# A sixth tile for the running block sums, earlier requests for block loads, four small buffers, and the fourth block's additions taken out of program order

## The chip, the cores and the metric

The kernel runs on one core of one Trainium2 chip. The metric is the time of one execution in microseconds (us), the median of several runs. Five engines of the core matter here: PE (TensorE, matrix products), ACT (ScalarE), DVE (VectorE), POOL (GpSimd, here mostly a queue that issues transfers, among them the ones that add to what lies in SBUF) and SP (SyncE, a second queue that issues transfers).

## The reference

One decoder layer on 256 tokens of width 2048, all in float32. The part that matters is the combined input projection:

```python
h = rmsnorm(x, pre_norm_g[l])
proj = h @ w_in[l]
(a_q, a_k, a_v, a_g, a_lr, b_q, b_k, b_v, b_g, m_a, m_b) = jnp.split(proj, offsets, axis=-1)
...
merged = jax.nn.sigmoid(m_a) * y_a + jax.nn.sigmoid(m_b) * y_b
out = merged @ w_out[l]
x = x + rmsnorm(out, post_norm_g[l])
```

The columns of `proj` feed a gated linear attention (`a_*`), a differential attention (`b_*`) and two merge gates (`m_*`). The two attentions give `y_a` and `y_b` by two further products with 2048 x 2048 weights.

## The kernel before

**Float32 as two halves.** Every weight tile is used as a rounded part `hi` and a remainder `lo`. In `emit_half` ACT writes `hi` (line 354, a copy that rounds, 128 x 1024) and DVE writes `lo` (line 355, the tile minus `hi`). PE multiplies `hi` with both parts of the activations and `lo` with the rounded part alone. One such pair of 128 x 1024 is called a half below. `hi`, `lo` and the raw tile each rotate through three buffers, and halves are prepared three ahead of PE (`AHEAD`, in `take`).

**The joined phase.** Nine stretches of 1024 columns (`SETS`, the sets 0 to 8) are not multiplied directly. Each is cut into four blocks of 1024 x 512 and computed with seven block products in place of eight. `PRODUCTS` gives their order: 1, 3, 5, 6, 2, 7, 4. Each block product has two parts `t` of two halves `h`, and a half takes six matmuls of 128 x 512. A block is held as two tiles of 128 x 2048 (1 MB), one for each `t`.

Some products need sums of blocks, and these are formed in place in running tiles (the tag `chain`, five buffers of 1 MB):

- the two tiles `a` are loaded with block 0 and used by product 1. Block 1 is then added by a transfer (`accumulate`, line 249, on POOL's queue) for product 5. Block 3 is then added by DVE out of the tiles `b` for product 6. Block 2 is added by DVE after that, for product 4.
- the two tiles `b` are loaded with block 3 and used by product 3. After DVE has added them to `a`, block 1 is added to them by a transfer, for product 7.
- block 2 alone is held in tiles `c`, which product 2 uses.

`follow_set` issues what follows a half. After the halves of product 5, part 1, it adds block 3 to the tile `a` of part 0; after those of product 6, part 0, to the tile `a` of part 1 (line 257; each addition is 128 x 1024). After the halves of product 7 the same line adds block 2. `emit_set` asks for the tiles of the next set through `link` (lines 222 to 228): `a` part 0 ahead of product 2, `a` part 1 ahead of product 7 part 1, `b` part 0 and `b` part 1 ahead of the two parts of product 4. A request takes a buffer of the tag; with five buffers and four in use by the set, the first request finds one free and each later one needs a buffer that the running set gives back.

**What runs beside the sets.** Between the halves of the sets come 64 halves of ordinary products (`others`): the last value columns, the keys and queries of the linear attention, and a part of those of the differential attention. `phase_steps` lists the order; a set takes 28 halves of its own and, from set 1 to set 7, seven of these. Small results wait in tiles `t2` (line 172, six buffers of 256 KB in this phase): sums of products (`p1`, `p5`, `p35`), and the queries and keys of the differential attention with their rounded parts (`dq`, `dk`, `dh`) until POOL has stored them.

**What sets the order of work.** Each engine runs its instructions in the order of its queue. That order is made ahead of time by a planner, which walks through the program with its own estimate of times. When an engine is free in that plan, it takes the instruction that comes first in the program among those whose inputs are ready. `keep_in_program_order` pins an instruction behind the one written just before it for the same engine. An instruction that isn't pinned may be taken ahead of others that are not ready yet. In `follow_set` all additions are pinned, and so are the transfers on POOL's queue. In the phase the matmuls are pinned too.

When the phase ends, the buffers of `blocks` and `first` (with `chain` and `t2`) are given up, and other pools take their space.

Of the kernel before, what the change touches and what calls it, by code (L numbers as in the profile page):

```python
# [6 lines left out]
F32 = mybir.dt.float32  # L7
# [4 lines left out]
ALU = mybir.AluOpType  # L12
AX = mybir.AxisListType

P = 128
# [127 lines left out]
def hybrid_kernel(ctx: ExitStack, tc, xt, xn, preg, postg, w, w2, gkb, glag, lamv, diffg, ident_d, causal_d, lmask_d, out):  # L143
    nc = tc.nc
    pe, act, dve, pool, sp = nc.tensor, nc.scalar, nc.vector, nc.gpsimd, nc.sync
# [8 lines left out]
    blocks = joint.enter_context(tc.tile_pool(name="blocks", bufs=2))  # L154
    pools = [joint.enter_context(tc.tile_pool(name="first", bufs=2))]
    count = [0]

    def u(shape, name, dtype=F32):
        count[0] += 1
        return big.tile(shape, dtype, tag="u", name=f"{name}_{count[0]}")  # L160
# [8 lines left out]

    def t2(shape, name):  # L170
        count[0] += 1
        return pools[0].tile(shape, F32, tag="t2", name=f"{name}_{count[0]}", bufs=6 if len(pools) == 1 else 12)

    def spill(t, name):
        count[0] += 1
# [13 lines left out]
    def f32(ap):  # L189
        return ap.bitcast(F32)  # L190
# [21 lines left out]
    raws = {}  # L212
    chain = {}
# [5 lines left out]
    def block(s, i, t):  # L219
        return weights(f"set{s}", 2 * i + t)[0]  # L220

    def link(s, name, t):
        count[0] += 1
        c = blocks.tile([P, 2048], F32, tag="chain", name=f"{name}_{count[0]}", bufs=5)
        i = (pool if s else sp).dma_start(c, block(s, {"a": 0, "b": 3}[name], t))
        if s:
            tc.keep_in_program_order(i)
        chain[s, name, t] = c

    def emit_set(s, prod, t, h):  # L230
        c = slice(1024 * h, 1024 * h + 1024)
        name, i = {(2, 0): ("a", 0), (7, 1): ("a", 1), (4, 0): ("b", 0), (4, 1): ("b", 1)}.get((prod, t), (None, 0))
        if h == 0 and name and s + 1 < SETS:
            link(s + 1, name, i)
        if h == 0 and s == 0 and prod == 1:
            link(s, "b", t)
        n = 4 * (PRODUCTS.index(prod) - PRODUCTS.index(2)) + 2 * t + h + LEAD
        if 0 <= n < 4:
            i, j = n // 2, n % 2
            raws[s, i, j] = u([P, 1024], "c")  # L240
            sp.dma_start(raws[s, i, j], block(s, 2, i)[:, 1024 * j : 1024 * j + 1024])
        a, b = chain[s, "a", t], chain[s, "b", t]
        return raws[s, t, h] if prod == 2 else (b if prod in (3, 7) else a)[:, c]

    def follow_set(s, prod, t, h):
        c = slice(1024 * h, 1024 * h + 1024)

        def accumulate(name, i):
            tc.keep_in_program_order(pool.dma_start(chain[s, name, i][:, c], block(s, 1, i)[:, c], accum_op=ALU.add))  # L249

        if prod == 1:
            accumulate("a", t)
        i = {(5, 1): 0, (6, 0): 1, (7, 0): 0, (7, 1): 1}.get((prod, t))
        if i is not None:
            a = chain[s, "a", i][:, c]
            second = prod != 7
            tc.keep_in_program_order(dve.tensor_tensor(out=a, in0=a, in1=chain[s, "b", i][:, c] if second else raws[s, i, h], op=ALU.add))  # L257
            if second:
                accumulate("b", i)

    def part_link(s, name, make=u2):
        first, second = {"b": (3, None), "f": (3, 1), "e": (1, 0)}[name]
        for h in range(2):
            c = slice(1024 * h, 1024 * h + 1024)
            t = chain[s, name, h] = make([P, 1024], f"part_{name}")
            tc.keep_in_program_order(sp.dma_start(t, weights(s, first)[0][:, c]))
            if second is not None:
                tc.keep_in_program_order(pool.dma_start(t, weights(s, second)[0][:, c], accum_op=ALU.add))
# [24 lines left out]
    def load(j):  # L293
        key, r, h = seq[j]
        src, size = weights(key, r)
        n = size // 2
        early = key == "v0"
        if key == "v3" and r == 0:
            for i in range(2):
                link(0, "a", i)  # L300
        count[0] += 1
        raw = raws[key, r] = wpool.tile([P, 2048], F32, tag="raw", name=f"raw_{count[0]}")
        cuts = (0, n, size) if j in (0, 2) else (0, size)
        for a, b in zip(cuts, cuts[1:]):
            i = sp.dma_start(raw[:, a:b], src[:, a:b])
            if early or key[0] == "o" or key in ("y10", "y11", "y12", "y13", "ys0"):
                tc.keep_in_program_order(i)
        if early and j // 2 in X_LOADS:
            load_x(*X_LOADS[j // 2])
# [12 lines left out]
    def emit_half():  # L322
# [10 lines left out]
        if e[0] == "part":  # L333
            r = chain[e[1], {3: "b", 7: "f"}.get(e[2], "e"), e[3]]
        else:
            r = emit_set(*e[1:]) if joined else emit_plain(j, *e)
# [19 lines left out]
        if joined:  # L356
            follow_set(*e[1:])
# [29 lines left out]
    def prep_x(kt):  # L387
# [4 lines left out]
        for i in (  # L392
# [3 lines left out]
            if kt < 2:  # L396
                tc.keep_in_program_order(i)

    ssum = t2([P, 512], "ssum")

    def square_x(i):
        src = xraw[i // 2][:, 2 * (i % 2) : 2 * (i % 2) + 2, :].rearrange("p a t -> p (a t)")
        t = t2([P, 512], "xsq") if i else ssum
        tc.keep_in_program_order(act.activation(t, src, AF.Square))
        if i:
            dve.tensor_tensor(out=ssum, in0=ssum, in1=t, op=ALU.add)
# [28 lines left out]
    ones = const.tile([P, P], F32, name="ones")  # L435
    dve.memset(ones, 1.0)
    ones_b = t2([P, BRIDGE], "ones_b").bitcast(BF16)[:, :BRIDGE]
    dve.memset(ones_b, 1.0)
    warm = ps("bg")
# [252 lines left out]
    def sum_operands():  # L692
        for kt in range(KT):
            x = xraw[kt // 4][:, kt % 4, :]
            act.activation(x, x, AF.Copy, scale=preg_s[:, kt : kt + 1])
            if kt % 4 == 3:
                yield
        temps = []
        for n in range(2):
            count[0] += 1  # L700
            temps.append(blocks.tile([P, 2, 8, P], F32, tag="chain", name=f"temp_{count[0]}", bufs=5))
        r1, s2, s4 = (temps[n // 2][:, n % 2] for n in range(3))

        def part(i, j, q):
            return xraw[2 * j + q][:, :, P * i : P * i + P]

        def rows(t, q):
            return t[:, 4 * q : 4 * q + 4]

        def split(name, t):  # L710
            hi, lo = (blocks.tile([P, 8, P], F32R, tag=f"{name}{e}", name=f"{name}{e}", bufs=1) for e in "hl")
            act.activation(hi, t, AF.Copy)
            dve.tensor_tensor(out=lo, in0=t, in1=f32(hi), op=ALU.subtract)
            sums[name] = hi, lo

        for q in range(2):
            dve.tensor_tensor(out=rows(r1, q), in0=part(1, 1, q), in1=part(1, 0, q), op=ALU.subtract)
            dve.scalar_tensor_tensor(out=rows(s2, q), in0=rows(r1, q), scalar=-1.0, in1=part(0, 0, q), op0=ALU.mult, op1=ALU.subtract)
        yield
        for q in range(2):  # L720
            dve.scalar_tensor_tensor(out=rows(s4, q), in0=rows(s2, q), scalar=-1.0, in1=part(0, 1, q), op0=ALU.mult, op1=ALU.subtract)
        split("s4", s4)
        yield
        split("r1", r1)
        yield
        split("s2", s2)

        def last_sum():
            r3 = u([P, 8, P], "r3")
            for q in range(2):  # L730
                dve.tensor_tensor(out=rows(r3, q), in0=part(0, 0, q), in1=part(1, 0, q), op=ALU.subtract)
            split("r3", r3)

        put_off.append(last_sum)
# [9 lines left out]
    tasks.append(late())  # L744
    tasks.append(forget_gate())
    tasks.append(sum_operands())
    start = 2 * VG[0] - RANK
    for g in (2, 3):
# [615 lines left out]
    def cell(b, g):  # L1364
        if (b, g // 2) not in yg:
            yg[b, g // 2] = u([P, 1024], "yg")
        return yg[b, g // 2][:, 512 * (g % 2) : 512 * (g % 2) + 512]
# [10 lines left out]
    def total(b, g, bank, i=None):  # L1378
        t = cell(b, g)
        tc.keep_in_program_order(dve.tensor_tensor(out=t, in0=bank, in1=t, op=ALU.add if left(g) else ALU.subtract))  # L1380
        if i is not None:
            square(b, t, 512, i)
            gain(b, t, 512 * g, 512)
        return t
# [160 lines left out]
    for g in (2, 3):  # L1545
# [7 lines left out]
        if g == 2:  # L1553
            total(0, 2, bank, 2)
            for b in range(2):
                xres.append([])
                for i in range(2):
                    t = u([P, 1024], "xres")
# [3 lines left out]
    t = total(0, 3, bank)  # L1562
# [10 lines left out]
    for c in range(2):  # L1573
# [6 lines left out]
        if c == 0:  # L1580
            t = cell(1, 3)[:, :256]
# [4 lines left out]
        else:  # L1586
            end = ps("bg")
            c = slice(TURNED[0] % 1024, TURNED[0] % 1024 + 512)
            t = yg[1, 1][:, c]
# [67 lines left out]
```

## Time and profile before

| | us |
|---|---|
| median of 3 runs (lowest to highest) | 1090.64 (1090.23 to 1091.9) |
| the profiled execution | 1089.85 |
| its span, from the first to the last instruction | 1088.0 |
| PE busy in the span | 1077.3 (99%) |
| DVE busy | 947.8 (87%) |
| ACT busy | 742.4 (68%) |
| POOL busy | 168.2 (15%) |

The joined phase runs from about 82 us to about 604 us of the span. Times of a timeline are counted from the start of the span. In a timeline or a chain a row has its start, its length, the engine, the line of the kernel and what it writes and reads; `[2.00 <-ACT hi L354]` says that the engine sat idle for 2.00 us just before, until the instruction named had finished. Matmul ends are modelled, and matmuls overlap in the pipeline, so a busy PE need not be at its full rate. The rate is better read from the distance between the starts of two matmuls.

### The profile page before, as it was taken

To read this page: it belongs to the slowest core of one execution; us is meant where nothing else is said; L and a number is where in the kernel's file an instruction comes from. 1 tells how busy PE (TensorE), PEld (TensorE's weight loads), DVE (VectorE), ACT (ScalarE), POOL (GpSimd) and SP (SyncE) were. 2 spreads that over 40 slices of the span, in tenths; PEclk is the share of its full clock that TensorE was granted. 3 is DMA by queue.
4 is the path that set the end of the run, shared out by engine and by line. 5 is a ranking of instruction groups with operands and counts; after the bars stand their busy time and mean duration, and the time that the engine had idled before them with its cause. 6 is when DMAs were issued, how large, how long until landed. Compare 5 with 4: busy or idle time off the path is not lost.

```text
span 1088.0 us, 15371 instructions
## 1 busy us (share of the span) xinstructions
PE 1077.3 (99%) x5404; PEld 918.0 (84%) x5404; DVE 947.8 (87%) x1282; ACT 742.4 (68%) x1068; POOL 168.2 (15%) x249
## 2 busy tenths in 40 slices
PE   9999999999999999999999999999999999999997
PEld 8998887878887888888888888888888888888886
DVE  7788989889998989898989899987778878879886
ACT  7987767777676767767776655566777776566662
POOL 0202121111212111212212210031011011100000
PEclk9999999999999999999999999999999999999999
DMA  8899799999897989898989776599897798988752
GB/s 347 271 340 285 226 288 283 256 269 300 230 344 173 358 184 374 197 335 218 316 240 273 273 258 202 194 321 315 277 299 257 272 297 269 325 300 260 273 190 99
DMA packets 67213, 293.44 MB, mean 270 GB/s; under 512 B 8704, under 2 KB 11776, under 8 KB 49984
## 3 DMA queue, kind: packets, MB, share of 16 engines
q1 hardware_dynamic: 38656, 174.29, 45.3%
q0 software_dynamic: 27904, 117.45, 40.2%
q8 instruction: 42, 0.69, 0.2%
q10 hardware_dynamic: 576, 0.73, 0.2%
q14 instruction: 35, 0.29, 0.1%
HBM read 265.17 MB, written 27.26 MB: 269 GB/s over the span
## 4 chain that ended last, share of the span: by engine, by line
PE 89%; DVE 5%; issue 2%; DMA 2%; ACT 1%; POOL 0%; POOLq 0%; SPq 0%; DVEq 0%; ACTq 0%
PE mm L551 60%; PE bg L551 18%; DVE lo L355 3%; PE mm L539 2%; PE bg L539 2%; DMA a<-in_w_dram 1%; DVE a L257 1%; PE mm L524 1%; PE bg L980 1%; PE bg L524 1%; PE bg L1147 0%; PE bg L1121 0%; DMA raw<-in_w_dram 0%; PE bg L1122 0%; PE bg L1159 0%
## 5 line engine op out<-in xcount | busy, mean ns | idle before, releaser
L354 ACT ACTIVATE hi<-raw 128x1024 fp32r<-128x1024 f32 (+3 forms) x229 | 234.6, 1028 | 148.9 <-PE mm L551 73.4
L355 DVE TENSOR_TENSOR lo<-raw,hi 128x1024 fp32r<-128x1024 f32 (+3 forms) x231 | 271.3, 1180 | 34.9 <-ACT hi L354 31.9
L354 ACT ACTIVATE hi<-a 128x1024 fp32r<-128x1024 f32 x144 | 152.5, 1060 | 63.1 <-PE mm L551 25.4
L355 DVE TENSOR_TENSOR lo<-a,hi 128x1024 fp32r<-128x1024 f32 x144 | 172.7, 1222 | 19.5 <-ACT hi L354 17.0
L551 PE MATMUL mm<-hi,xs 128*128 128x512 f32 (+1 forms) x688 | 174.8, 383 | 0.0
L551 PEld LDWEIGHTS mm<-hi,xs 128*128 128x128 f32 x688 | 128.5, 188 | 21.4
L551 PE MATMUL bg<-xs,hi 128*128 128x512 f32 x448 | 115.7, 390 | 0.0
L355 DVE TENSOR_TENSOR lo<-b,hi 128x1024 fp32r<-128x1024 f32 x72 | 88.0, 1223 | 18.0 <-ACT hi L354 15.9
L551 PE MATMUL mm<-lo,xs 128*128 128x512 f32 (+1 forms) x344 | 98.7, 383 | 0.1
L551 PEld LDWEIGHTS bg<-xs,hi 128*128 128x128 f32 x448 | 84.3, 188 | 16.6
L354 ACT ACTIVATE hi<-b 128x1024 fp32r<-128x1024 f32 x72 | 76.1, 1060 | 25.5 <-PE mm L551 13.5
L551 PE MATMUL mm<-xs,hi 128*128 128x512 f32 x320 | 84.9, 397 | 0.0
L551 PEld LDWEIGHTS mm<-lo,xs 128*128 128x128 f32 x344 | 64.2, 188 | 12.2 <-DVE lo L355 1.3
L551 PEld LDWEIGHTS bg<-xs,lo 128*128 128x128 f32 x448 | 60.3, 190 | 10.5 <-DVE lo L355 6.8
L551 PE MATMUL bg<-xs,lo 128*128 128x256 f32 x448 | 63.5, 285 | 2.6 <-DVE lo L355 2.4
L551 PEld LDWEIGHTS mm<-xs,hi 128*128 128x128 f32 x320 | 57.7, 189 | 9.6
L249 POOL DMA_DIRECT2D b<-in_w_dram x36 | 31.0, 861 | 169.1 <-ACT hi L354 70.1
L354 ACT ACTIVATE hi<-c 128x1024 fp32r<-128x1024 f32 x36 | 38.2, 1062 | 21.0 <-PE bg L551 9.7
L551 PE MATMUL mm<-hi,oah 128*128 128x512 f32 x128 | 50.9, 397 | 0.0
L551 PE MATMUL mm<-hi,oal 128*128 128x512 f32 x128 | 50.1, 391 | 0.0
L551 PEld LDWEIGHTS mm<-xs,lo 128*128 128x128 f32 x320 | 43.7, 190 | 3.2
L551 PE MATMUL mm<-xs,lo 128*128 128x256 f32 x320 | 44.6, 283 | 0.0
(410 smaller groups left out, 2218.6 us busy)
## 6 DMA issues: line engine op xcount, KB each, us to landing
raw<-in_w_dram SPq DMA_DIRECT2D x98, 1024.0 KB, 7.0
c<-in_w_dram SPq DMA_DIRECT2D x36, 512.0 KB, 8.4
a<-in_w_dram POOLq DMA_DIRECT2D x36, 512.0 KB, 9.8
b<-in_w_dram POOLq DMA_DIRECT2D x36, 512.0 KB, 8.4
a<-in_w_dram POOLq DMA_DIRECT2D x16, 1024.0 KB, 10.6
b<-in_w_dram POOLq DMA_DIRECT2D x16, 1024.0 KB, 7.9
raw<-in_w_dram SPq DMA_DIRECT2D x14, 832.0 KB, 7.1
gr<-gr POOLq DMA_DIRECT2D x9, 512.0 KB, 10.1
```

The lines of the kernel that those rows point to most:

```text
L249: tc.keep_in_program_order(pool.dma_start(chain[s, name, i][:, c], block(s, 1, i)[:, c], accum_op=ALU.add))
L257: tc.keep_in_program_order(dve.tensor_tensor(out=a, in0=a, in1=chain[s, "b", i][:, c] if second else raws[s, i, h], op=ALU.add))
L354: act.activation(hi_t[:, a:b], r[:, a:b], AF.Copy)
L355: dve.tensor_tensor(out=lo_t[:, a:b], in0=r[:, a:b], in1=f32(hi_t[:, a:b]), op=ALU.subtract)
L524: i = pe.matmul(out, lhs, rhs, start=first and n == 0, stop=last and n == len(pairs) - 1, **kw)
L539: i = pe.matmul(banks[g][b][:, :n], a[part][:, P * b : P * b + P], w[:, n * g : n * g + n], start=first, stop=last)
L551: i = pe.matmul(*args, **kw)
L980: pe.matmul(o, xk[:, P * c : P * c + P], xq.rearrange("p (b c t) -> p b c t", b=2, c=4)[:, :, c, :], start=i == 0, stop=i == 1)
```

## The change

The tag `chain` gets a sixth buffer. The requests for the next set's tiles move: `a` part 1 is asked for ahead of product 7 part 0, `b` part 0 ahead of product 7 part 1, `b` part 1 ahead of product 4 part 0. The tiles `t2` get four buffers in place of six as long as the joined phase and what precedes it run. The additions of block 3 to `a` (those after products 5 and 6) are no longer pinned; the additions of block 2 (after product 7) stay pinned. What is computed is the same.

```diff
     def t2(shape, name):
...
-        return pools[0].tile(shape, F32, tag="t2", name=f"{name}_{count[0]}", bufs=6 if len(pools) == 1 else 12)
+        return pools[0].tile(shape, F32, tag="t2", name=f"{name}_{count[0]}", bufs=4 if len(pools) == 1 else 12)
...
     def link(s, name, t):
...
-        c = blocks.tile([P, 2048], F32, tag="chain", name=f"{name}_{count[0]}", bufs=5)
+        c = blocks.tile([P, 2048], F32, tag="chain", name=f"{name}_{count[0]}", bufs=6)
...
     def emit_set(s, prod, t, h):
...
-        name, i = {(2, 0): ("a", 0), (7, 1): ("a", 1), (4, 0): ("b", 0), (4, 1): ("b", 1)}.get((prod, t), (None, 0))
+        name, i = {(2, 0): ("a", 0), (7, 0): ("a", 1), (7, 1): ("b", 0), (4, 0): ("b", 1)}.get((prod, t), (None, 0))
...
             second = prod != 7
-            tc.keep_in_program_order(dve.tensor_tensor(out=a, in0=a, in1=chain[s, "b", i][:, c] if second else raws[s, i, h], op=ALU.add))
+            add = dve.tensor_tensor(out=a, in0=a, in1=chain[s, "b", i][:, c] if second else raws[s, i, h], op=ALU.add)
             if second:
                 accumulate("b", i)
+            else:
+                tc.keep_in_program_order(add)
...
-            temps.append(blocks.tile([P, 2, 8, P], F32, tag="chain", name=f"temp_{count[0]}", bufs=5))
+            temps.append(blocks.tile([P, 2, 8, P], F32, tag="chain", name=f"temp_{count[0]}", bufs=6))
```

## The prediction

> **What bounds the kernel now.** I read the page first, then the chain of waits in order of time, then the timelines of DVE and PE in the places where that chain leaves PE.
>
> ```profile
> PE 89%; DVE 5%; issue 2%; DMA 2%; ACT 1%; POOL 0%; POOLq 0%; SPq 0%; DVEq 0%; ACTq 0%
> ```
>
> PE carries 89% of the chain, so the bound is PE's own matmuls. A change that leaves the matmuls alone can win only the places where PE waits. The joined phase shows them by its period. The chain lists one unbroken PE piece of 48 matmuls per set (product 4 and the next set's product 1):
>
> ```profile
> 196.46 10.90 PE mm L551 x48
> ...
> 255.34 10.91 PE mm L551 x48
> ...
> 312.98 10.90 PE mm L551 x48
> ...
> 372.19 10.91 PE mm L551 x48
> ...
> 429.83 10.90 PE mm L551 x48
> ...
> 489.43 10.91 PE mm L551 x48
> ...
> 547.67 10.90 PE mm L551 x48
> ```
>
> From one start to the next the sets 2 to 7 take 58.88, 57.64, 59.21, 57.64, 59.60 and 58.24 us. They hold the same matmuls, so 57.64 (sets 3 and 5) is a set without a wait, and the others lose 1.24 (set 2), 1.57 (set 4), 1.96 (set 6) and 0.60 (set 7). In the chain, set 2's loss looks like this:
>
> ```profile
> 230.74 1.14 DVE lo L355
> ...
> 231.92 1.45 PE bg L551 x9
> ```
>
> PE waits for a `lo` that DVE finishes late. DVE's timeline shows the cause:
>
> ```profile
> 219.49 1.23 DVE L355 TENSOR_TENSOR lo<-a,hi 128x1024 fp32r<-128x1024 f32 x1 [2.00 <-ACT hi L354]
> 220.63 1.22 DVE L257 TENSOR_TENSOR a<-a,b 128x1024 f32<-128x1024 f32 x1
> ...
> 223.24 1.22 DVE L257 TENSOR_TENSOR a<-a,b 128x1024 f32<-128x1024 f32 x1
> ...
> 226.64 1.22 DVE L257 TENSOR_TENSOR a<-a,b 128x1024 f32<-128x1024 f32 x1
> ...
> 228.91 1.22 DVE L257 TENSOR_TENSOR a<-a,b 128x1024 f32<-128x1024 f32 x1
> ...
> 230.65 1.22 DVE L355 TENSOR_TENSOR lo<-raw,hi 128x1024 fp32r<-128x1024 f32 x1
> ```
>
> DVE sits idle for 2.00 us up to 219.49. From there it works without a gap, and the last row's `lo` is the one that PE waits for. Four additions of block 3 stand in that stretch. Each displaces the queue by 1.13 or 1.14 (220.63 less 219.49, for a row of the same length). The idle time and the burst are neighbours.
>
> **The change part by part.** (1) *The unpinned additions.* No instruction is added or removed: 36 additions of block 3 may move up. The first pair (`a` part 0) is written after the halves of product 5 part 1, but reads `a` part 0, last read by product 5 part 0, and `b`, which product 3 used long before. So its inputs are ready one part earlier, before the `lo` at 219.49, while DVE sits idle. A free engine takes the earliest ready instruction of the program; waiting for 219.49's `hi` it has nothing else. I expect both additions of the pair in this gap. They take 2 x 1.13 = 2.26 where 2.00 is idle, and push the `lo` back by about 0.3. That `lo` isn't urgent: PE's wait comes twelve us later. The burst then holds two additions fewer, 2.0 us net, against a loss of 1.24. The second pair (`a` part 1) becomes ready inside the burst, where DVE always has an earlier ready instruction; I leave it in place. The same gap stands in the other sets with a loss, and half of it in a set without:
>
> ```profile
> 102.30 1.23 DVE L355 TENSOR_TENSOR lo<-a,hi 128x1024 fp32r<-128x1024 f32 x1 [0.68 <-ACT hi L354]
> ...
> 163.42 1.23 DVE L355 TENSOR_TENSOR lo<-a,hi 128x1024 fp32r<-128x1024 f32 x1 [1.49 <-ACT hi L354]
> ...
> 277.42 1.23 DVE L355 TENSOR_TENSOR lo<-a,hi 128x1024 fp32r<-128x1024 f32 x1 [1.03 <-ACT hi L354]
> ...
> 336.02 1.23 DVE L355 TENSOR_TENSOR lo<-a,hi 128x1024 fp32r<-128x1024 f32 x1 [2.00 <-ACT hi L354]
> ...
> 452.87 1.23 DVE L355 TENSOR_TENSOR lo<-a,hi 128x1024 fp32r<-128x1024 f32 x1 [2.00 <-ACT hi L354]
> ```
>
> Set 4 (336.02) has 2.00 us of idle time against 1.57 of loss: all of it goes. Set 6 (452.87) has the same 2.00, so I take the same 1.57 for it; I count the other 0.39 of its 1.96 as not won.
>
> ```profile
> 544.33 0.69 DVE L887 TENSOR_TENSOR gr<-mm,p 128x512 f32<-128x512 f32 x1
> ```
>
> Sets 3 and 5 (277.42 is set 3's) have nothing to win. Set 7's 0.60 stands behind the `gr` of 544.33, after product 7, so I count none of it. Set 8 has six ordinary halves, one fewer:
>
> ```profile
> 600.30 2.77 PE bg L551 x16
> 603.07 27.22 PE mm L551 x120
> ```
>
> From 547.67 to 603.07 it takes 55.40, where 57.64 less 2.77 is 54.87: 0.5 lost. Set 0, with 0.68 idle at 102.30, may lose as much in the same place. I leave both out, since their gaps are smaller than an addition. So (1) gives 1.24 + 1.57 + 1.57 = 4.4 us. Its bounds: 0 if the planner leaves the additions where they are, and 4.4 + 0.39 + 0.60 + 0.5 + 0.5 = 6.4 if all goes. Below nothing: an addition taken too early delays one `lo` by 1.13, while the burst's last `lo` still comes after the same work. So it can cost only where nothing is lost now, one displacement in each of the sets 3, 5 and 7: 3.4.
>
> The addition's follower, the transfer that adds block 1 to `b` (line 249, POOL's queue), may go up to 3 us sooner; product 7 doesn't wait for it now.
>
> (2) *The sixth tile and the earlier requests.* Before, the second request stood in POOL's queue until a `b` tile was given back:
>
> ```profile
> 174.02 0.55 POOL L225 DMA_DIRECT2D a<-in_w_dram  x1
> 186.10 0.54 POOL L225 DMA_DIRECT2D a<-in_w_dram  x1 [11.53 <-DVE lo L355]
> 192.45 0.54 POOL L225 DMA_DIRECT2D b<-in_w_dram  x1 [5.80 <-DVE lo L355]
> ```
>
> With a sixth buffer `a` part 1 goes right behind `a` part 0 (174.5 in place of 186.10), `b` part 0 takes the place at 186.1, `b` part 1 that at 192.45. Each still waits only for a tile that was waited for at that place before, so nothing new is queued behind a wait, and what stands behind in POOL's queue (stores of `k`, `q`, `dh`, `dl`, the transfers of line 249) has one wait fewer ahead of it. Only once does PE lose time to a transfer of this family, in set 1:
>
> ```profile
> 146.68 15.54 DMA a<-in_w_dram
> ```
>
> ```profile
> a<-in_w_dram POOLq DMA_DIRECT2D x36, 512.0 KB, 9.8
> ```
>
> ```profile
> 136.95 1.09 PE L551 MATMUL mm<-hi,xs 128*128 128x512 f32 x4
> 138.11 0.73 PE L551 MATMUL mm<-lo,xs 128*128 128x512 f32 x2
> ...
> 196.29 1.09 PE L551 MATMUL mm<-hi,xs 128*128 128x512 f32 x4
> 197.22 0.62 PE L551 MATMUL mm<-lo,xs 128*128 128x512 f32 x2
> ```
>
> From 136.95 to 196.29 set 1 takes 59.34, 1.70 over 57.64. The first 0.34 falls at 138.11, ahead of the late transfer (1.16 and 0.73 there, 0.93 and 0.62 at 197.22). The rest, 1.36, begins with it: 15.54 us from issue to landing, where the page's median of these is 9.8. Two loads of 1 MB stand just ahead of it in the same queue; one of them now goes ten us sooner. I take 1.3 for this term, since the gap of 1.49 at 163.42 also lets additions be drawn ahead. Bounds 0 and 1.36.
>
> ```profile
> 148.00:163.00 15.00, 15.00 (x75) 12.73 (x74) 10.96 (x11) 8.73 (x10) 0.54 (x1) 1.00 1.03 287
> ```
>
> In that stretch the transfer engines are busy throughout (share 1.03). The Trainium skill ("DMA: Bandwidth & Descriptors", section "Issuing engines are not separate DMA queues") says that transfers of all queues run on the same 16 engines and interleave. By that rule asking sooner only shifts the load, the late transfer could stay late, and the sum would lose this term. The trace agrees that the engines are full there; it doesn't show whether they would be with 1 MB less.
>
> (3) *Four buffers for `t2`.* A buffer too few would stop ACT or DVE until POOL has stored a tile. From set 5 on the users are `p5`, `p35`, one `dq` or `dk`, and its `dh`: four. A fifth is wanted when the next `dq` or `dk` starts before the last is stored:
>
> ```profile
> 474.21 0.54 POOL L177 DMA_DIRECT2D dl<-dk  x1 [0.39 <-issue]
> ...
> 542.28 0.54 POOL L177 DMA_DIRECT2D dl<-dk  x1 [0.52 <-DVE dk L772]
> ...
> DMA to landing us min/median/max: 2.9/4.1/8.3
> ```
>
> ```profile
> 484.92 0.37 ACT L764 ACTIVATE dq<-bg 128x256 f32<-128x256 f32 x1
> ...
> 548.67 0.37 ACT L764 ACTIVATE dq<-bg 128x256 f32<-128x256 f32 x1
> ```
>
> The next tile starts 10.7 and 6.4 us after the stores were issued. At both times `p35` is already dead, so a fourth buffer is free even with both stores in flight. Cost nothing; if that cover is gone, see the slower rival.
>
> **The sum.** 4.4 + 1.3 = 5.7 us. Against the profiled execution, 1089.85 (span 1088.0 and 1.85 around it), that gives 1084.15. The runs' median lies 0.79 above that execution, so I forecast 1084.9.
>
> **The rivals.**
>
> *The planner leaves the additions in place.* In its own estimate DVE may have no gap before the `lo` of product 5 part 1. For it: the plan's times aren't the chip's. Against it: the gap comes from ACT waiting for PE to free a `hi` buffer, which any estimate near the chip's has. Then only the second term is left at most: 1089.3 to 1090.6, no change that counts.
>
> *Half of it.* Additions move up in some sets, or only one of a pair: 1.13 of 2.26 us. With one of a pair the sets 2, 4 and 6 keep 0.1, 0.4 and 0.4, and the late transfer may stay too, 1.3: 1085.8 to 1087.1; with additions moved in one set of the three, 1088.
>
> *All of it.* Sets 0, 7 and 8 win too, and set 0's run of waits around product 7 with them: 1090.64 less 6.4, less 1.36, and less four waits like the 0.34 at 138.11 (an estimate, since set 0 has no period to compare) is 1081.5.
>
> *Slower, by the small buffers.* POOL's queue now has two 1 MB loads back to back ahead of the stores of `dk` and `dh`. The moved 1 MB takes 3.7 us of the stretch quoted above at its 287 GB/s. A store that lands in 8.3 now would then take 12.0. If the plan has put the next `dq`, `dh` or `p5` on that buffer, ACT's write waits, and with it every `hi` queued behind it on ACT. Three prepared halves cover 4.1 us (18 of 48 matmuls in 10.90), so one such place costs up to 7.9; at three places (sets 6, 7 and 8) a third to a half of that each gives 8 to 12, less 5.7, and 1093 to 1097. It decides only if five `t2` tiles are alive at once. Against it: the rows above show four.
>
> **How the numbers follow.** The forecast has a chance of 0.50, half of it 0.14, all of it 0.11, no change 0.16, slower 0.09. About 0.2% (2.2 us) is what a measurement of this kernel can tell from no change, so faster means below 1088.46. The first three cases lie there, less a little at the edge of the second: 0.73. Same is 0.18 with that edge, slower 0.09. The range reaches from "all of it", 1081.5, to the middle of the two cases above the forecast, 1091.5; outside are about half of "all of it" and most of the slower rival, 0.14 in all.
>
> **What would show it.** Right: in DVE's timeline of sets 2, 4 and 6 the rows `a<-a,b` stand ahead of the `lo` that answers to 219.49, the gap of 2.00 is gone, and PE's pieces of 48 matmuls lie 57.6 to 57.8 apart in sets 2 and 4. The second request of line 225 follows the first at once, and the landing time of 15.54 falls to 13 or less. No wait of ACT on a store appears. Wrong: the order of DVE's rows is as before, or the gap is filled and PE's pieces are as far apart as before; or additions stand ahead of urgent `lo`s and sets 3 and 5 grow beyond 57.64.

## The result, and the profile after

The changed kernel takes **1082.95 us** (median; 1082.61 to 1083.89) beside 1090.74 us before: a ratio of 0.9928, 95% interval 0.9911 to 0.9946. The forecast was 1084.9. The profiled execution took 1083.89 us, 5.96 less than that of before, with a span of 1082.1.

The joined phase in the chain of waits, after. Ahead of the pieces of 48 stands a piece at the start of set 0, behind them the piece that ends the phase:

```profile
94.18 5.49 PE mm L553 x24
...
194.66 10.90 PE mm L553 x48
...
252.28 10.91 PE mm L553 x48
...
309.92 10.90 PE mm L553 x48
...
367.55 10.91 PE mm L553 x48
...
425.19 10.90 PE mm L553 x48
...
483.18 10.91 PE mm L553 x48
...
540.82 10.90 PE mm L553 x48
...
595.77 27.22 PE mm L553 x120
...
719.04 12.37 DMA vback<-vl
```

The same early piece before (the other rows of that chain stand in the prediction):

```profile
94.23 5.49 PE mm L551 x24
```

The differences of these starts give the length of each set. "Sets 0, 1" runs from the early piece to the first piece of 48, and set 8 from the last of these to the piece of 120:

| us | sets 0, 1 | set 2 | 3 | 4 | 5 | 6 | 7 | 8 |
|---|---|---|---|---|---|---|---|---|
| before | 102.23 | 58.88 | 57.64 | 59.21 | 57.64 | 59.60 | 58.24 | 55.40 |
| after | 100.48 | 57.62 | 57.64 | 57.63 | 57.64 | 57.99 | 57.64 | 54.95 |

Every loss that the prediction named has gone, but for 0.35 in set 6, a part of set 0 and 0.08 in set 8. The phase ends 7.30 us sooner (603.07 less 595.77), and 1.4 of that is lost again behind the phase. Most of it (about 1.0) is the last row of the fence: a fetch of linear-attention values lands after 12.37 us, and PE waits for it.

That fetch also changes the share of the chain by engine. The page after:

```profile
PE 85%; issue 8%; DVE 3%; DMA 2%; POOL 1%; ACT 0%; POOLq 0%; SPq 0%; DVEq 0%; ACTq 0%
```

PE fell from 89% to 85% although its waits shrank. Followed back from the late fetch, the chain runs through the queue that issued it and not through PE, though PE was as busy. A share of the chain is no measure of a gain; the distance between PE's pieces is.

DVE's timeline in set 2, after:

```profile
213.11 1.23 DVE L357 TENSOR_TENSOR lo<-a,hi 128x1024 fp32r<-128x1024 f32 x1
214.37 1.23 DVE L257 TENSOR_TENSOR a<-a,b 128x1024 f32<-128x1024 f32 x1
215.51 1.22 DVE L357 TENSOR_TENSOR lo<-a,hi 128x1024 fp32r<-128x1024 f32 x1
216.76 1.22 DVE L257 TENSOR_TENSOR a<-a,b 128x1024 f32<-128x1024 f32 x1
217.91 1.22 DVE L357 TENSOR_TENSOR lo<-a,hi 128x1024 fp32r<-128x1024 f32 x1
...
222.78 1.22 DVE L257 TENSOR_TENSOR a<-a,b 128x1024 f32<-128x1024 f32 x1
...
225.05 1.22 DVE L257 TENSOR_TENSOR a<-a,b 128x1024 f32<-128x1024 f32 x1
```

The 2.00 us of idle time are gone. The first two additions stand each behind one half of product 5 part 0 (213.11, 215.51). The `lo` that had waited stands 23.25 us behind the set's first row (217.91 less 194.66), where it stood at 23.03 (219.49 less 196.46): pushed back by 0.22, about the 0.3 that was expected. The second pair has stayed among the halves that follow.

### The profile page after: what moved, and what is told of

The parts are those of the page before. It is cut to its first block, busy times and chain, and to the rows that moved or that the text cites. A ratio compares the mean times of both kernels' runs of the same rounds, so it can differ in the third digit from the quotient of the medians.

```text
span 1082.1 us, 15375 instructions
## 1 busy us (share of the span) xinstructions
PE 1073.0 (99%) x5404; PEld 919.1 (85%) x5404; DVE 948.0 (88%) x1282; ACT 741.8 (69%) x1068; POOL 168.1 (16%) x249
## 4 chain that ended last, share of the span: by engine, by line
PE 85%; issue 8%; DVE 3%; DMA 2%; POOL 1%; ACT 0%; POOLq 0%; SPq 0%; DVEq 0%; ACTq 0%
PE mm L553 57%; PE bg L553 20%; PE mm L541 2%; PE bg L541 2%; DVE lo L357 2%; DMA vback<-vl 1%; DMA raw<-in_w_dram 1%; PE bg L1149 0%; PE bg L1123 0%; PE bg L526 0%; PE bg L1124 0%; POOL dl L177 0%; DVE keep L357 0%; PE bg L1161 0%; PE bg L1162 0%
## 5 line engine op out<-in xcount | busy, mean ns | idle before, releaser
L357 DVE TENSOR_TENSOR lo<-c,hi 128x1024 fp32r<-128x1024 f32 x36 | 43.1, 1219 | 5.0 <-ACT hi L356 5.0
```

What stands on the lines that cost most here:

```text
L357: dve.tensor_tensor(out=lo_t[:, a:b], in0=r[:, a:b], in1=f32(hi_t[:, a:b]), op=ALU.subtract)
```

## The experiments

The experiments ran on three chips: the first four on one, the next four on a second, the last four on a third. Each ratio is against runs of the kernel before on the same chip, and "the run beside it" is one of the same chip. Set lengths are differences of starts as above, each from one profiled execution.

**The additions alone.**

```diff
 # before
-            tc.keep_in_program_order(dve.tensor_tensor(out=a, in0=a, in1=..., op=ALU.add))
+            add = dve.tensor_tensor(out=a, in0=a, in1=..., op=ALU.add)
             if second:
                 accumulate("b", i)
+            else:
+                tc.keep_in_program_order(add)
```

> Before with one part of the change: the additions of block 3 unpinned; five tiles, six small buffers and the old places of the requests stay. Theory A (the additions carry all but set 1, the sixth tile carries set 1): the phase's last piece of 120 matmuls starts at 603.07 less 5.9 = 597.1, sets 2, 4, 6, 7 and 8 are as short as in the changed kernel, set 1 keeps its 1.36; median about 1084.6. Theory B (the earlier requests also shorten sets 2 to 8, through POOL's queue and the transfers): at most the 4.4 of sets 2, 4 and 6 is won, 598.7 or later, median 1086.3 or more. Theory C (set 1's wait goes because additions are drawn ahead of it, the tile does nothing): 595.8, median 1083.

Measured: 1084.55 us, ratio 0.9942 (0.9929 to 0.9956). The chain:

```profile
93.31 5.49 PE mm L553 x24
...
145.37 16.33 DMA a<-in_w_dram
...
195.20 10.90 PE mm L553 x48
...
596.30 27.22 PE mm L553 x120
```

From 195.20 to 596.30 the sets 2 to 8 take 401.10, where they took 406.61 before and 401.11 with the whole change. So all that these sets won, 5.5 us, comes from the additions. The last piece starts 0.8 us ahead of theory A's 597.1, which is no more than this execution was ahead at set 0 (93.31 for 94.23). Set 1's late transfer is still there, 16.33 us. Theories B and C fall.

**The sixth tile alone.**

```diff
 # the changed kernel
-            add = dve.tensor_tensor(out=a, in0=a, in1=..., op=ALU.add)
+            tc.keep_in_program_order(dve.tensor_tensor(out=a, in0=a, in1=..., op=ALU.add))
             if second:
                 accumulate("b", i)
-            else:
-                tc.keep_in_program_order(add)
```

> The changed kernel with the additions of block 3 pinned again: sixth tile, new places of the requests, four small buffers. Theory A: only set 1's late transfer goes, the last piece of 120 matmuls starts at 603.07 less 1.3 = 601.8, median about 1089.4, sets 2, 4, 6 keep 1.2 to 2.0 us each. Theory B: 600.5 or earlier, median 1088 or less. Theory C (asking sooner only shifts load on the same transfer engines): 603.1, median 1090.7, and the transfer of set 1 still lands after 15 us.

Measured: 1088.16 us, 0.9972 (0.9962 to 0.9982).

```profile
93.35 5.49 PE mm L551 x24
...
194.45 10.90 PE mm L551 x48
...
600.88 27.22 PE mm L551 x120
```

Sets 2 to 8 take 406.43, as before (406.61), and no transfer of set 1 stands in the chain: theory A, though its median (1089.4) was too high. Sets 0 and 1 take 101.10 in place of 102.23, so the tile with the new places is worth 1.13 there. The median fell by more, 2.5; the run with four small buffers (below) shows a likely reason.

**The sixth tile with the old places of the requests.**

```diff
 # the kernel above
-        name, i = {(2, 0): ("a", 0), (7, 0): ("a", 1), (7, 1): ("b", 0), (4, 0): ("b", 1)}.get((prod, t), (None, 0))
+        name, i = {(2, 0): ("a", 0), (7, 1): ("a", 1), (4, 0): ("b", 0), (4, 1): ("b", 1)}.get((prod, t), (None, 0))
```

> As the run with the tile alone, but with the requests at their old places in the program; the sixth tile and four small buffers stay, additions pinned. In POOL's queue the order is then that of before, and the sixth tile takes away one wait for a returned tile. Theory A1 (the tile, not the place, moves the request): the second request follows the first at once, the same time as the run with the tile alone, within 0.3 us. Theory A2 (the place matters): set 1's wait stays, about 1090.7.

Measured: 1089.84 us, 0.9990 (0.9981 to 0.9999), 1.7 above the run before; in the profiled executions sets 0 and 1 take 101.66 against 101.10. POOL's queue in set 0, of this kernel:

```profile
112.48 1.41 POOL L225 DMA_DIRECT2D a<-in_w_dram  x2
...
136.25 0.54 POOL L177 DMA_DIRECT2D vl<-vl  x1 [4.55 <-DVE vl L674]
136.78 1.08 POOL L225 DMA_DIRECT2D b<-in_w_dram  x2
```

The tile alone moves the second request (`x2`: two at once). The first request for `b` still stands behind the stores of `vh` and `vl`, whose data ACT and DVE finish late. With the new places it is ahead of them, as the changed kernel's row shows:

```profile
127.36 0.54 POOL L225 DMA_DIRECT2D b<-in_w_dram  x1 [13.42 <-DVE lo L357]
```

What that does to the transfer engines is in the windows (busy time of each engine, granted clock, the share of the 16 transfer engines, GB/s) before, with the tile and the new places, and with the tile and the old places:

```profile
124.00:136.00 12.00, 11.62 (x53) 9.05 (x51) 12.00 (x13) 8.72 (x12) 1.10 (x2) 1.00 0.55 186
```

```profile
124.00:136.00 12.00, 11.61 (x55) 9.04 (x54) 12.00 (x14) 8.72 (x11) 1.08 (x2) 1.00 0.69 252
```

```profile
124.00:136.00 12.00, 11.61 (x55) 9.04 (x55) 12.00 (x14) 8.72 (x11) 0.54 (x1) 1.00 0.44 160
```

The stretch from 148 to 163 is full in all three (share 1.03 or 1.04). Some way ahead of it, from 124 to 136, the engines were about half idle before (0.55; 0.62 in the run below, which has the same order). With the old places the tile leaves that hole emptier (0.44), with the new ones a megabyte goes there, and between hole and full stretch, from 136 to 148, the share falls from 0.88 before to 0.77 (0.86 with the old places). The chain of this run has no transfer in set 1 either. But the last of the four transfers of that place takes 15.0 from issue to landing where it took 14.5, ACT's `hi` that needs it starts at 160.79 instead of 160.33, and DVE's queue reaches the `lo` for which PE waits as much later.

So neither theory holds alone. How much is the tile and how much the place stays open: in the profiles the place gives 0.56, in the medians 1.7 of the 2.5, and the profiled execution of this run was the fastest of its eleven (1088.15).

**Four small buffers alone.**

```diff
 # before
-        ..., bufs=6 if len(pools) == 1 else 12)
+        ..., bufs=4 if len(pools) == 1 else 12)
```

> Before with four small buffers in place of six and nothing else. Theory A (four are enough, the cost is nothing): 603.07 for the last piece of 120 matmuls within 0.2, median 1090.7 within 0.5. Rival (a store comes too late for the next small result and ACT or DVE waits): 1093 to 1097, with ACT or DVE idle on a small tile in sets 6 to 8.

Measured: 1090.23 us, 0.9995 (0.9987 to 1.0004): nothing. Each engine's instructions stand in the same order as before. So this run also shows how one and the same program differs from one execution to the next:

```profile
93.27 5.49 PE mm L551 x24
...
145.69 16.49 DMA a<-in_w_dram
...
196.42 10.90 PE mm L551 x48
```

It reached set 0 0.96 sooner than the profiled execution of before (93.27 against 94.23), yet set 2 at the same time (196.42 against 196.46). Set 1's transfer lands at 162.18 (145.69 + 16.49) here and at 162.22 before, though it was issued 0.99 sooner here. With five tiles the early start was lost at that transfer; with six it is kept: the changed kernel takes the same time for sets 0 and 1 whether it starts them at 94.18 (100.48) or at 93.61 (100.47, the run below). Against this run the tile with the new places is worth 2.05 there (103.15 less 101.10), which fits the 2.5 in the median better than 1.13.

In sets 0 and 1 the two parts also overlap. Against this run the additions alone win 1.26 (103.15 less 101.89), the tile with the new places 2.05, and both together 2.67 (103.15 less 100.48), so what is put down to one depends on whether the other is there.

**The changed kernel once more**, with no edit.

> The changed kernel once more, unedited, on the chip of the runs beside it. It tells whether the wait for vback at 719 us of the first profile (about 1.0 us of the chain) belongs to the change. Theory A (it is the luck of one execution's transfers): the chain has no vback row, the last piece of 120 matmuls starts at 595 to 596 and the span is about 1081. Theory B (the change causes it): the row is there again, the span 1082.

Measured: 1082.42 us, 0.9929 (0.9916 to 0.9942), sets 0 to 7 within 0.01 and set 8 within 0.03 of the first profile. The late fetch is there again (at 718.43, landing after 11.81). It costs about 0.4 here and about 1.0 in the first profile. Its row isn't in the chains of the additions alone, of the first pair left out or of block 2 sooner in set 0 (below), which issue these fetches in the same order; it is in that of block 2 sooner in two sets, which does so too. The runs without it speak against theory B, and two profiles out of two of this kernel speak for it; what decides it stays open.

**The additions in three sets alone.**

```diff
 # the changed kernel
             if second:
                 accumulate("b", i)
-            else:
+            if not second or s not in (2, 4, 6):
                 tc.keep_in_program_order(add)
```

> The changed kernel with the additions of block 3 unpinned in sets 2, 4 and 6 alone, as the prediction's first term counted them; pinned in the other sets. Theory A (each set wins by itself, and sets 0, 7 and 8 win too): sets 2, 4 and 6 as short as in the changed kernel (57.62, 57.63, 57.99), sets 7 and 8 keep 0.60 and 0.45 and set 0 its 0.4, so the median is 1.4 above the changed kernel's. Theory B (sets 7 and 8 win because the sets before them end earlier): they are short here too, and the median is within 0.5 of the changed kernel's.

Measured: 1084.11 us, 0.9941 (0.9929 to 0.9953), 1.7 above the kernel beside it. Sets 2, 4 and 6 are as short as with the whole change (57.62, 57.63, 57.99). Sets 7 and 8 are not:

```profile
482.95 10.91 PE mm L553 x48
...
541.19 10.90 PE mm L553 x48
...
596.45 27.22 PE mm L553 x120
```

Set 7 has its 58.24 back, set 8 takes 55.26, and sets 0 and 1 take 100.86 in place of 100.48. Each set wins by itself (theory A); the additions in sets 0, 7 and 8 give 0.38, 0.60 and 0.31. The first of these is small beside the spread: the kernel with the tile alone has the same order up to set 2, and took 101.10 for sets 0 and 1 where this one took 100.86. It can be seen in set 0 by itself, though: its piece of 36 matmuls starts 20.70 behind the early piece here (114.27 less 93.57) and 20.28 in the changed kernel (114.46 less 94.18).

**The first pair left out.**

```diff
 # the changed kernel
+        if (prod, t) == (5, 1):
+            accumulate("b", 0)
-        if i is not None:
+        elif i is not None:
```

> The changed kernel with the first pair of block 3's additions left out in every set (18 additions of 1.14 us; the second pair and all transfers stay), so the values are not the reference's. Theory A (a moved addition lies in idle time and costs nothing): sets 2 to 5 and 7 stay at 57.6, only the remnants of set 6 (0.35) and set 0 can fall, median 0 to 0.8 below the changed kernel's. Theory B (the moved additions still cost part of their 2 x 1.14 somewhere in the set): 0.3 us or more in each of sets 1 to 8, median 2.4 or more below.

Measured: 1082.68 us, 0.9927 (0.9916 to 0.9939), against 1082.42 beside it.

```profile
93.64 5.49 PE mm L555 x24
...
194.13 10.90 PE mm L555 x48
...
540.30 10.90 PE mm L555 x48
```

DVE does 18 additions less, some 20 us of work, and PE gains nothing: sets 0 and 1 take 100.49 (100.48 with them), sets 2 to 7 346.17 (346.16). So in its new place the first pair is free, and block 3's first pair has no part in the 0.35 left in set 6 (58.00 here).

**Block 2's first pair sooner, in sets 0 and 6.**

```diff
 # the changed kernel
-        i = {(5, 1): 0, (6, 0): 1, (7, 0): 0, (7, 1): 1}.get((prod, t))
+        early = s in (0, 6)
+        i = {(5, 1): 0, (6, 0): 1, (2, 1) if early else (7, 0): 0, (7, 1): 1}.get((prod, t))
...
-            second = prod != 7
+            second = prod in (5, 6)
```

> The changed kernel, with the first pair of block 2's additions written behind product 2, part 1, in place of product 7, part 0, in sets 0 and 6 alone. There DVE sits idle for 1.45 us (set 0) and 0.83 to 1.1 us ahead of product 7, and a burst without a gap behind it makes PE wait in product 7 and after it (about 1.6 us in set 0, 0.34 in set 6). Theory A (the same mechanism as block 3's: the burst is what PE waits for): set 0's waits fall by 1.0 to 1.6 and set 6's by 0.3, median 1.0 to 1.9 below the changed kernel's. Theory B (set 0's waits come from the small values on ACT and DVE there, not from the number of additions): no change. Theory C (the additions delay product 2's own halves): slower by up to 1.

Measured: 1081.98 us, 0.9927 (0.9915 to 0.9940). Sets 0 and 1 take 98.97, 1.51 less. Set 6 takes 59.14 in place of 57.99:

```profile
423.09 10.90 PE mm L554 x48
...
465.27 0.40 DVE a L258
...
466.41 1.23 DVE lo L358
...
482.23 10.91 PE mm L554 x48
```

Theory A holds in set 0 and C in set 6. My reading of set 6 was wrong: its idle time of 0.83 stands ahead of product 2, not behind it. From there DVE works without a gap, so the addition at 465.27 delayed a half for which PE was already waiting in the changed kernel.

**Block 2's first pair sooner, in set 0 alone.**

```diff
 # the changed kernel
-        i = {(5, 1): 0, (6, 0): 1, (7, 0): 0, (7, 1): 1}.get((prod, t))
+        i = {(5, 1): 0, (6, 0): 1, (7 if s else 2, 1 - (s > 0)): 0, (7, 1): 1}.get((prod, t))
...
-            second = prod != 7
+            second = prod in (5, 6)
```

The new key is `(2, 1)` in set 0 and `(7, 0)`, as before, in every other set.

> The changed kernel, with the first pair of block 2's additions written behind product 2, part 1, in set 0 alone (the run before did it in sets 0 and 6; set 0 won 1.57 of its waits, and set 6 grew from 57.99 to 59.14). Theory A (the two effects are separate): set 0 wins 1.57 again, set 6 is back at 57.99, the last piece of 120 matmuls starts 1.5 to 1.6 sooner than in the changed kernel and the median is about 1080.9, faster than both kernels. Theory B (what set 0 wins is taken back by set 1's transfers): 1082.4.

Measured: **1080.49 us**, 0.9902 (0.9886 to 0.9919), the lowest median of all. Sets 0 and 1 take 98.94, set 6 is back at 57.99, and the phase ends at 593.54:

```profile
93.50 5.49 PE mm L553 x24
...
192.44 10.90 PE mm L553 x48
...
593.54 27.22 PE mm L553 x120
```

**The same, with the third pair of vback fetches asked for sooner.**

```diff
 # the run above
         bring(1)
+        bring(2)
         yield
         while "scores1" not in done:
             yield
-        bring(2)
```

> As the run beside it, and the third pair of vback fetches is written ahead of the stores of dh and dl that it followed in POOL's queue (it was issued at 718.5 and needed 11.8 us later). Theory A (this transfer sits at the edge and decides part of the executions): no vback row in the chain, the median 0.3 to 1.0 below the run beside it, the runs closer together. Theory B (other transfers decide the rest of the spread): the same median within 0.3.

Measured: 1080.68 us, 0.9905 (0.9889 to 0.9922): no difference. As the run beside it shows no vback row either, this doesn't tell whether the edit would help an execution that has one.

**Both pairs of block 3 sooner.**

```diff
 # the changed kernel; besides this, every addition is pinned here
-        i = {(5, 1): 0, (6, 0): 1, (7, 0): 0, (7, 1): 1}.get((prod, t))
+        i = {(5, 0): 0, (5, 1): 1, (7, 0): 0, (7, 1): 1}.get((prod, t))
```

> The changed kernel with all additions pinned, but block 3's written one part sooner in the program, both pairs: part 0 behind product 5 part 0, part 1 behind product 5 part 1. The prediction held that the second pair may stay in place. Theory A (the burst is short enough once the first pair is gone): sets 2 to 5 and 7 stay at 57.6, set 6 keeps 0.3, the median within 0.4 of the changed kernel's. Theory B (an addition written ahead of a half that PE needs soon delays it): some sets grow by 0.3 to 1.1 each, the median 1 to 4 above. Theory C (the second pair still costs something): up to 0.8 below.

Measured: 1089.11 us, 0.9992 (0.9980 to 1.0005). The gain is gone. Sets 2 to 7 take 58.15, 57.98, 58.47, 57.99, 58.83 and 58.45. The chain in set 2:

```profile
219.77 1.21 DVE a L257
...
220.99 1.15 DVE lo L355
```

Here the first pair stands as in the changed kernel, and an addition of the second pair (219.77) stands ahead of the `lo` that PE waits for (220.99). Theory B.

**Block 2's additions left to the planner.**

```diff
 # the changed kernel
-            else:
-                tc.keep_in_program_order(add)
```

> The changed kernel with block 2's additions unpinned too, so that the planner places them; it draws one of each first pair ahead of product 2's own halves. Theory A (what the planner draws into a real gap is free, as with block 3): set 0 wins 1.0 to 1.6, the other sets stay at 57.6, median about 1081. Theory B (here the plan's gaps are not the chip's: DVE has halves to do that PE needs, as in set 6 of the run with block 2 sooner): sets 1 to 8 grow by 0.3 to 1.2 where an addition stands ahead of a half, median 1083 to 1090.

Measured: 1081.54 us, 0.9911 (0.9895 to 0.9927). Sets 0 and 1 take 98.91, but set 2 grows from 57.62 to 58.42, and sets 4, 6 and 7 by 0.05 to 0.11. In set 2's chain PE waits for product 2's own half, with two of the unpinned additions ahead of it in DVE's queue (first row: those two, from the timeline; then the chain):

```profile
228.17 2.35 DVE L257 TENSOR_TENSOR a<-a,c 128x1024 f32<-128x1024 f32 x2
```

```profile
232.58 1.14 DVE lo L355
```

Both theories hold in part. The planner's gap was real on the chip in set 0 and not in set 2.

## Why the prediction was right, and where not

**The bound and the sets' losses: right.** The sets with a loss are the ones that shrank, and sets 3 and 5 didn't move.

**The first term, 4.4: right in size.** Sets 2, 4 and 6 won 1.26, 1.58 and 1.61, together 4.45, and did so with the other sets pinned. That both additions would stand in one gap was wrong: each took the place behind one half of part 0. The idle time was filled all the same. That the second pair stays in place was right, and the run with both pairs sooner shows that it had to: moved up by one part (and pinned there), it costs all the gain.

**What wasn't counted: wrong.** The step that failed is "I leave both out, since their gaps are smaller than an addition", and with it set 7, whose 0.60 "stands behind the `gr` of 544.33". Sets 7, 8 and 0 won 0.60, 0.45 and 0.38, 1.43 in all. (In set 8 the run with set 8 pinned kept 0.31 of its 0.45.)

In sets 0 and 8 a gap smaller than an addition paid all the same. Set 0 had 0.68 of idle time at 102.30. Drawn ahead of it, an addition (1.13) moves the queue behind it up by what was idle (here 0.86: the 0.68 and a shorter pause), whether it fits or not: the next `lo` of an ordinary half stands 17.80 behind the early piece (111.98 less 94.18), where it stood at 18.66 (112.89 less 94.23), and PE's wait of about 0.4 there is gone. In set 8 the idle time was in pieces too short for the timeline to mark: three `lo` in a row took 3.94 (from 564.76), where three without a gap take 3.49; now an addition stands among them (559.17), and PE's wait behind them is gone.

Set 7 is another matter. DVE before, then after:

```profile
543.03 1.22 DVE L257 TENSOR_TENSOR a<-a,c 128x1024 f32<-128x1024 f32 x1
544.33 0.69 DVE L887 TENSOR_TENSOR gr<-mm,p 128x512 f32<-128x512 f32 x1
544.94 1.22 DVE L355 TENSOR_TENSOR lo<-raw,hi 128x1024 fp32r<-128x1024 f32 x1
```

```profile
536.74 1.22 DVE L257 TENSOR_TENSOR a<-a,c 128x1024 f32<-128x1024 f32 x1
537.88 1.22 DVE L357 TENSOR_TENSOR lo<-raw,hi 128x1024 fp32r<-128x1024 f32 x1
539.01 0.68 DVE L889 TENSOR_TENSOR gr<-mm,p 128x512 f32<-128x512 f32 x1
```

DVE's queue is no further ahead: the addition stands 53.60 behind the set's start before (543.03 less 489.43) and 53.56 after (536.74 less 483.18). What changed is the order behind it. Before, `gr`, which the kernel writes under `tc.high_priority`, needs the last matmul of product 7 (PE's piece ends at 544.31) and stands ahead of the `lo` that PE needs next; it displaces that `lo` by 0.61 (544.94 less 544.33), and PE loses 0.60. After, the planner has put the `lo` first. In the run with three sets, where set 7's additions are pinned, `gr` is ahead again and the 0.60 is back. So the prediction named the right wait, and missed that unpinning an addition can also change the order in which the planner takes other instructions, 30 us later. Why the plan turned out that way isn't shown; the trace has the chip's times, not the plan's.

**Set 6's remainder: right to leave out, with a size of 0.35 for 0.39.** A second gap (0.83) lies between the additions of block 3 and that wait, so what is won ahead of it doesn't reach it.

**The second term, 1.3: right in size, and its mark missed.** Sets 0 and 1 won 1.75 (102.23 less 100.48), and without the additions' 0.38 that is 1.37. On top of the additions the tile and the new places give 1.41 (101.89 less 100.48). But against the run with four small buffers, which reached set 0 earlier, they are worth 2.05 by themselves, more than the bound of 1.36. That bound came from one profile, so that the size fits this well is in part luck. The landing was to fall from 15.54 to 13 or less. Of the four transfers of this family in that place, after:

```profile
DMA to landing us min/median/max: 5.4/10.1/14.3
```

The slowest still takes 14.3. That was enough: the last is issued at 146.21, so all have landed by 160.5 instead of 162.2, and no transfer of set 1 stands in PE's chain. The Trainium skill ("DMA: Bandwidth & Descriptors", section "Issuing engines are not separate DMA queues") says that transfers from all queues interleave on the same 16 engines. The runs agree with that; but from it the rival followed only if the engines were full beforehand too, and they were at 0.55 between 124 and 136.

**The third term, 0: right** (0.9995).

**The sum.** 5.7 was expected and 7.30 came at the end of the phase: 5.82 for the two terms and 1.43 for what wasn't counted make 7.25; the other 0.05 is the earlier start (94.18 for 94.23). In the profiled execution, the slowest of its four, 1.4 went again behind the phase; the medians differ by 7.8, so other executions probably keep more. Of the rivals, "all of it" (1081.5, a chance of 0.11) came nearer than the forecast: it is 1.45 off the measured time, the forecast (1084.9) 1.95. Its condition that sets 0, 7 and 8 win too was met. What kept it from being right is set 0's run of waits, which the change left in place and which the move of block 2's pair removed.

## What to carry to other kernels

Where PE waits for an engine that works through its queue in order, follow that queue back from the wait to its last idle gap, and stop where a row waits for PE itself: work drawn ahead of a gap pays the gap's length, up to the loss, even if it doesn't fit, and work drawn past a half that PE is about to need takes back what was won. Then compare the order of the rows next to the wait, before and after: a planner that gets one more freedom may also swap instructions that nobody touched. Before an earlier request is priced, look at the transfer engines' share ahead of the late transfer as well as at it; here it paid, with a hole to fill. A planner's freedom is worth taking where its gaps are the chip's, and has to be checked set by set.

## What the runs showed of the hardware that was not expected

The same order of instructions reached the early piece of set 0 at 93.27 in one execution and at 94.23 in another, and the early one was no faster at set 2 (196.42 and 196.46): the transfer at the end of the full stretch landed at 162.2 in both. The landing of one and the same fetch of 512 KB behind the phase took 12.37 and 11.81 us in two profiles of one kernel, and 14.51 in the run with block 2 sooner in two sets, where PE lost some 4.5 us to it.
